# A bilinear einsum on one core: the last weight loads cut by group instead of by pairs of groups

## The chip, the cores and the metric
The kernel runs on one core of one Trainium2 chip. The metric is device time in microseconds (us). Before the change it is a median of 86.06 us over 8 runs, from 85.73 to 86.56. The profile was taken of one execution of 85.89 us, whose span from first to last instruction is 84.6 us.

## The reference
```python
batch, dim_i, dim_j, dim_k = 32, 256, 256, 128        # all float32
out[b, k] = sum over i, j of x[b, i] * y[b, j] * weight[k, i, j]
# np.einsum('bi,bj,kij->bk', x, y, weight)
```
The weight is 128 x 256 x 256 floats, 33.6 MB; x, y and the output are small. So every weight is read once from HBM and used for 32 batches.

## The kernel before, in words
**Layout.** The 128 values of k are split into 32 groups (G) of four: group g holds k = kk * 32 + g for kk from 0 to 3. The 256 values of i are split as i = ip * 8 + ic, with ip from 0 to 31 and ic from 0 to 7. A partition of SBUF holds one pair (ip, kk), 128 in all. In a partition, a group is a row of 8 x 256 values, column block ic holding the 256 values of j for that i. In HBM such a row is contiguous, 8 KB of float32; the load casts it to bf16, so it takes 4 KB in SBUF. A whole group is 1 MB in HBM and 512 KB in SBUF. The profile's sizes of loads are those in SBUF.

**Loads.** Groups 0 and 16 (FIRST) come as float32 on SyncE's queue and are cast by ScalarE. All other groups come through the DMA queue of GpSimd (POOL), in the order of the table LOADS (lines 17 to 31). An entry (groups, lo, hi) is one DMA (line 150): for each of these groups, the column blocks lo to hi - 1 of all 128 partitions. It has one descriptor row for each partition and group, of (hi - lo) x 256 values, and its own semaphore, which all 16 DMA engines raise. All loads are issued in one go near the start, with no wait between them, and wait in the queue in that order. The first five entries are whole rows of 2, 4, 8, 8 and 4 groups. The last eight entries bring groups 7, 23, 15 and 31 in column pieces.

**Units.** UNITS (lines 9 to 15) cuts the 32 groups into five units of 16, 8, 4, 2 and 2 groups, and TensorE works through them in this order. For each column block ic it multiplies xblk, which holds x for this ic on a mask by kk, so that the 128 output rows are the pairs (b, kk), with the weights; PSUM accumulates over the eight ic. In the first four units a matmul takes two groups at once (512 columns). In the last unit, groups 15 and 31, each matmul takes one group (256 columns). Units alternate in the direction in which they run over ic; unit (7, 23) runs from ic 7 down to 0, the last from 0 up. The list `steps` (lines 254 to 256) holds the order of matmuls of a unit as (ic, h, o), where h is the place in PSUM and o the group in the unit. Before a matmul, TensorE waits for the semaphores of the loads which bring its operands, if it has not waited for them before (lines 259 to 275). Every wait holds up all that stands behind it on TensorE.

**Behind TensorE.** VectorE multiplies the sums of a unit by y (line 285) and reduces over j (line 289). In the last unit it does both in one instruction for each group (line 294): the first begins when TensorE has raised s_pe after the last matmul of group 15, the second after the last of group 31 (line 276). Then SyncE sends out the 16 KB of results (line 303), and GpSimd clears the semaphores.

Of the kernel before, what the change touches and what calls it, by code (L numbers as in the profile page):

```python
# [19 lines left out]
    (tuple(range(2, 32, 4)), 0, 8),  # L20
    (tuple(range(1, 32, 4)), 0, 8),
    ((3, 11, 19, 27), 0, 8),
    ((7, 23), 4, 8),
    ((7, 23), 0, 4),
    ((15, 31), 0, 3),
    ((15, 31), 3, 5),
    ((15, 31), 5, 6),
    ((15,), 6, 8),
    ((31,), 6, 7),
    ((31,), 7, 8),  # L30
)
# [6 lines left out]
def kernel(  # L38
# [20 lines left out]
    IC = I // IP  # L59
# [113 lines left out]
    def done(ins):  # L173
        nonlocal n_dve
        n_dve += 1
        ins.then_inc(s_dve, 1)
        return n_dve
# [45 lines left out]
    def product(out, lhsT, rhs, first, last, load):  # L223
        return pe.add_instruction(mybir.InstMatmult(  # L224
            name=nc.get_next_instruction_name(), engine=mybir.EngineType.PE,
            ins=[pe.lower_ap(rhs), pe.lower_ap(lhsT)], outs=[pe.lower_ap(out)],
            start_tensor_calc=first, stop_tensor_calc=last,
            tile_size=(P, P), tile_position=(0, 0), ldweights=load,
        ))
# [9 lines left out]
    for u, unit in enumerate(UNITS):  # L239

        n_g = len(unit)
        last = u == len(UNITS) - 1
        n_b = n_g if last else n_g // 2
        if bank + n_b > BANKS:
            bank = 0
        free = max(freed[bank:bank + n_b])
        if free > at_dve:
            pe.wait_ge(s_dve, free)
            at_dve = free

        up = (len(UNITS) - 1 - u) % 2 == 0
        order = range(IC) if up else range(IC - 1, -1, -1)

        steps = [(ic, h, n_g // n_b * h) for ic in order for h in range(n_b)]
        if last:
            steps = steps[:12] + [(6, 0, 0), (7, 0, 0), (6, 1, 1), (7, 1, 1)]
        for n_step, (ic, h, o) in enumerate(steps):
            n = n_g // n_b
            need = []
            for g in unit[o:o + n]:  # L260
                s = sem_of.get((g, ic))
                if s is not None and s.num not in landed:
                    landed.add(s.num)
                    need.append(s)
            for s in need[:-1]:
                pe.wait_ge(s, 16)
            c = product(
                ps[:, bank + h, :n, :],
                xblk[:, ic, :, :].rearrange("p b kk -> p (b kk)"),
                w_sb[:, p0 + o:p0 + o + n, ic * J:(ic + 1) * J],  # L270
                first=(ic == order[0]), last=(ic == order[-1]), load=(held != ic),
            )
            held = ic
            if need:
                c._wait_ge(need[-1], 16)
            if n_step == len(steps) - 1 or (last and n_step == len(steps) - 3):
                n_pe += 1
                c.then_inc(s_pe, 1)
        prod = tmp[:, u % 2, :n_g, :]
        if last:  # L280
            sums = ps[:, bank:bank + n_g, 0, :]
        else:
            sums = ps[:, bank:bank + n_b, :, :].rearrange("p a h j -> p (a h) j")
        if not last:
            t = done(v.tensor_tensor(  # L285
                out=prod, in0=sums, in1=y4.unsqueeze(1).to_broadcast([P, n_g, J]), op=mult,
            )._wait_ge(s_pe, n_pe))
            freed[bank:bank + n_b] = [t] * n_b
            done(v.tensor_reduce(  # L289
                out=acc[:, unit[0]:unit[-1] + 1:unit[1] - unit[0]], in_=prod, axis=AX, op=add,  # L290
            )._wait_ge(s_dve, t))
        else:
            for n, g in enumerate(unit):
                done(v.tensor_tensor_reduce(  # L294
                    out=prod[:, n, :], in0=sums[:, n, :], in1=y4, scale=1.0, scalar=0.0,
                    op0=mult, op1=add, accum_out=acc[:, g:g + 1],
                )._wait_ge(s_pe, n_pe - 1 + n))
        bank += n_b
        p0 += n_g
# [40 lines left out]
```

## Time and profile before
| What | Before |
|---|---|
| time, median of 8 runs | 86.06 us (85.73 to 86.56) |
| profiled execution, and its span | 85.89 us, 84.6 us |
| TensorE matmul, busy | 34.3 us, 136 instructions |
| VectorE, busy | 24.9 us |
| POOL, busy | 10.7 us |
| HBM read | 33.62 MB, 398 GB/s over the span |
| DMA packets | 5728, of them 5200 on POOL's queue |
| packets under 512 B / 2 KB / 8 KB | 416 / 1632 / 5472 |

Busy time of an engine is the sum over its instructions; TensorE's matmuls are pipelined, so it is no measure of how near TensorE is to its limit. A packet's size is counted as it is written to SBUF. The rate in GB/s of a slice or window counts bytes written too, so a load that casts from float32 to bf16 reads twice that rate from HBM. TensorE's granted clock is about half in three of the page's 40 slices, from 61.3 to 67.7 us.

### The profile page before, as it was taken

Reading aid. Unit: us, or ns where it says so; the run is one execution under the profiler, and the core shown is the slowest. Engines: PE = TensorE matmul, PEld = TensorE weight load, DVE = VectorE, ACT = ScalarE, POOL = GpSimd, SP = SyncE. Lnnn points to the kernel's source line nnn. Section 1 sums busy time; section 2 is a strip of 40 time slices with the busy share of each in tenths; the row PEclk is TensorE's granted clock in tenths of the full one; section 3 lists DMA queues with packets and bytes.
Section 4 is the critical chain, followed back from the end, with each engine's and each line's share of the span. In section 5 each row is a group of like instructions: output and inputs, shape, how many; then the busy total and the mean of one; then the engine's idle time right before and its main releaser. Section 6 shows DMA issues by size and latency. Waiting matters only on the chain.

```text
span 84.6 us, 277 instructions
## 1 busy us (share of the span) xinstructions
PE 34.3 (41%) x136; PEld 3.8 (5%) x38; DVE 24.9 (29%) x28; ACT 5.3 (6%) x5; POOL 10.7 (13%) x19
## 2 busy tenths in 40 slices
PE   0000000000000000000099999998009999999560
PEld 0000000000000000000000000000000011123110
DVE  0799600000000000000000000000999910499962
ACT  0637700000000000000000000000000000000000
POOL 0599994000000000000000000000000000000000
PEclk9999999999999999999999999999955589999999
DMA  4999999999999999999999999999999999999940
GB/s 97 409 405 256 215 217 217 215 217 213 215 217 213 215 215 209 211 217 217 215 217 217 215 213 217 215 217 215 211 209 211 217 217 208 192 209 206 193 57 8
DMA packets 5728, 17.91 MB, mean 212 GB/s; under 512 B 416, under 2 KB 1632, under 8 KB 5472
## 3 DMA queue, kind: packets, MB, share of 16 engines
q0 software_dynamic: 5200, 15.73, 94.5%
q1 hardware_dynamic: 432, 2.11, 6.7%
q10 hardware_dynamic: 96, 0.07, 0.3%
HBM read 33.62 MB, written 0.02 MB: 398 GB/s over the span
## 4 chain that ended last, share of the span: by engine, by line
DMA 44%; PE 41%; DVE 6%; POOL 2%; issue 2%; another core or an unknown queue 2%; POOLq 0%
DMA w_sb<-in_weight_dram 44%; PE ps L224 41%; DVE tmp L285 5%; POOL w_sb L150 1%; DVE tmp L294 1%; POOL ident L156 0%; POOL ident L155 0%; POOLq L134 0%; DVE acc L294 0%
## 5 line engine op out<-in xcount | busy, mean ns | idle before, releaser
L224 PE MATMUL ps<-w_sb,xblk 128*128 128x512 bf16 (+1 forms) x136 | 34.3, 414 | 48.3 <-DMA w_sb<-in_weight_dram 43.6
L285 DVE TENSOR_TENSOR tmp<-ps,y 128x4096 f32<-128x4096 f32 (+3 forms) x4 | 8.6, 2153 | 54.2 <-PE ps L224 54.2
L150 POOL DMA_DIRECT2D w_sb<-in_weight_dram x13 | 10.0, 777 | 2.6 <-POOLq L134 2.6
L289 DVE TENSOR_REDUCE acc<-tmp 128x16 f32<-128x4096 f32 (+3 forms) x4 | 8.6, 2154 | 0.1
L224 PEld LDWEIGHTS ps<-w_sb,xblk 128*128 128x128 bf16 x38 | 3.8, 103 | 78.6 <-DMA w_sb<-in_weight_dram 44.7
L165 ACT CAST w_sb<-w_f 128x1024 bf16<-128x1024 f32 x4 | 4.0, 1042 | 2.3 <-DMA w_f<-in_weight_dram 2.3
L214 DVE STREAM_TRANSPOSE y<-y_rep 32x256 f32<-32x256 f32 x4 | 1.7, 435 | 0.1
L185 DVE STREAM_TRANSPOSE xt<-x_rep 32x256 f32<-32x256 f32 x4 | 1.7, 434 | 0.1
L197 DVE TENSOR_SCALAR xblk<-xt,mask 128x256 bf16<-128x256 f32 x4 | 1.5, 524 | 0.0
L179 DVE COPY x_rep<-x_sb 32x1024 f32<-32x1024 f32 x1 | 0.7, 681 | 2.6 <-PEq L134 2.6
L165 ACT ACT_TABLE_LOAD x1 | 1.3, 1283 | 2.6 <-PEq L134 2.6
L294 DVE CUSTOM_DVE_ANT_0 tmp<-ps,y 128x256 f32<-128x256 f32 x2 | 0.8, 424 | 0.8 <-PE ps L224 0.8
L209 DVE COPY y_rep<-yt 32x1024 f32<-32x1024 f32 x1 | 0.7, 694 | 0.0
L206 DVE STREAM_TRANSPOSE yt<-y_sb 32x256 f32<-32x256 f32 x1 | 0.4, 426 | 0.0
L192 DVE TENSOR_REDUCE mask<-ident 128x4 f32<-128x128 f32 x1 | 0.4, 376 | 0.1
L156 POOL TENSOR_SCALAR_AFFINE_SELECT ident<-ident 128x128 f32<-128x128 f32 x1 | 0.3, 287 | 0.1
L155 POOL MEMSET ident<- 128x128 f32 x1 | 0.2, 223 | 0.0
L294 DVE DVE_READ_ACCUMULATOR2_ANT acc<- 128x1 f32 x2 | 0.2, 83 | 0.0
L324 POOL MEMSET const-float32-0.0<- 128x1 f32 x1 | 0.1, 98 | 0.2 <-issue 0.2
L324 POOL MEMSET const-bfloat16-1.0<- 128x1 bf16 x1 | 0.1, 101 | 0.0
L324 POOL MEMSET const-uint8-127<- 128x1 uint8 x1 | 0.1, 101 | 0.0
L324 POOL MEMSET const-float32-1.0<- 128x1 f32 x1 | 0.1, 98 | 0.0
## 6 DMA issues: line engine op xcount, KB each, us to landing
w_sb<-in_weight_dram POOLq DMA_DIRECT2D x2, 4096.0 KB, 46.2
w_sb<-in_weight_dram POOLq DMA_DIRECT2D x2, 2048.0 KB, 41.2
w_f<-in_weight_dram SPq DMA_DIRECT2D x2, 1024.0 KB, 6.5
w_sb<-in_weight_dram POOLq DMA_DIRECT2D x1, 1024.0 KB, 9.7
w_sb<-in_weight_dram POOLq DMA_DIRECT2D x2, 512.0 KB, 66.7
w_sb<-in_weight_dram POOLq DMA_DIRECT2D x1, 384.0 KB, 68.8
w_sb<-in_weight_dram POOLq DMA_DIRECT2D x1, 256.0 KB, 69.4
w_sb<-in_weight_dram POOLq DMA_DIRECT2D x2, 128.0 KB, 69.5
```

The costliest lines, as they stand in the source:

```text
L150: pool.dma_start(out=w_of(groups)[:, :, lo * J:hi * J], in_=rows_of(groups)[:, :, lo * J:hi * J],).then_inc(s, 16)
L165: c = act.copy(out=w_sb[:, place_of[g], lo:hi], in_=w_f[:, n, lo:hi])
L179: t = done(v.tensor_copy(out=x_rep, in_=x_sb.rearrange("b (ip ic) -> b ic ip", ic=IC).unsqueeze(3) .to_broadcast([B, IC, IP, KK]),)._wait_ ...
L185: c = v.transpose(out=xt[q * 32:(q + 1) * 32, :, :], in_=x_rep[:, :, q * IP // Q:(q + 1) * IP // Q, :],)
L192: t = done(v.tensor_reduce(out=mask, in_=ident.rearrange("p (ip kk) -> p kk ip", kk=KK), axis=AX, op=add,)._wait_ge(s_pool, 2))
L197: c = v.tensor_scalar(out=xblk[:, :, :, kk], in0=xt, scalar1=mask[:, kk:kk + 1], scalar2=None, op0=mult,)
L209: t = done(v.tensor_copy(out=y_rep, in_=yt.unsqueeze(3).to_broadcast([B, J // 32, B, KK]),)._wait_ge(s_dve, t))
L214: c = v.transpose(out=y4[q * 32:(q + 1) * 32, :].rearrange("p (jb j) -> p jb j", j=32), in_=y_rep[:, :, q * BQ:(q + 1) * BQ, :],)
L224: return pe.add_instruction(mybir.InstMatmult(name=nc.get_next_instruction_name(), engine=mybir.EngineType.PE, ins=[pe.lower_ap(rhs), pe.l ...
L285: t = done(v.tensor_tensor(out=prod, in0=sums, in1=y4.unsqueeze(1).to_broadcast([P, n_g, J]), op=mult,)._wait_ge(s_pe, n_pe))
L289: done(v.tensor_reduce(out=acc[:, unit[0]:unit[-1] + 1:unit[1] - unit[0]], in_=prod, axis=AX, op=add,)._wait_ge(s_dve, t))
L294: done(v.tensor_tensor_reduce(out=prod[:, n, :], in0=sums[:, n, :], in1=y4, scale=1.0, scalar=0.0, op0=mult, op1=add, accum_out=acc[:, g:g ...
```

## The change
The first five loads stay. The other eight become ten: each of them brings columns of one group alone, four column blocks at a time for groups 7, 23, 15 and for the first half of 31; the second half of 31 comes as two blocks, one and one. The order of TensorE in the last unit is fitted to this: ic 0 to 3 for both groups in turn, then ic 4 to 7 of group 15, then ic 4 to 7 of group 31. The signal to VectorE that group 15 is done moves with it, from the third matmul before the end to the fifth, both counted so that the last is the first. Arithmetic, bytes and the number of matmuls stay as they are.

```diff
@@ LOADS
     ((3, 11, 19, 27), 0, 8),
-    ((7, 23), 4, 8),
-    ((7, 23), 0, 4),
-    ((15, 31), 0, 3),
-    ((15, 31), 3, 5),
-    ((15, 31), 5, 6),
-    ((15,), 6, 8),
+    ((7,), 4, 8),
+    ((23,), 4, 8),
+    ((7,), 0, 4),
+    ((23,), 0, 4),
+    ((15,), 0, 4),
+    ((31,), 0, 4),
+    ((15,), 4, 8),
+    ((31,), 4, 6),
     ((31,), 6, 7),
     ((31,), 7, 8),
 )
@@ tile_einsum_bilinear_kernel
         if last:
-            steps = steps[:12] + [(6, 0, 0), (7, 0, 0), (6, 1, 1), (7, 1, 1)]
+            steps = steps[:8] + [(ic, h, h) for h in range(2) for ic in range(4, IC)]
@@
-            if n_step == len(steps) - 1 or (last and n_step == len(steps) - 3):
+            if n_step == len(steps) - 1 or (last and n_step == len(steps) - 5):
```

## The prediction
> **What bounds the kernel now.** I read four views of the kernel before: the page's chain by line, the chain in order of time, the windows around the landings, and the waits. The page says that weight loads and TensorE share the chain almost evenly:
>
> ```profile
> span 84.6 us, 277 instructions
> DMA w_sb<-in_weight_dram 44%; PE ps L224 41%; DVE tmp L285 5%; POOL w_sb L150 1%; DVE tmp L294 1%; POOL ident L156 0%; POOL ident L155 0%; POOLq L134 0%; DVE acc L294 0%
> ```
>
> That share misleads about the end. In order of time, the last stretch of the chain reads (start us, duration us, what):
>
> ```profile
> 75.85 2.38 PE ps L224 x11
> 78.22 0.44 another core or an unknown queue
> 78.66 0.04 issue
> 78.70 0.81 PE ps L224 x6
> 79.52 0.47 another core or an unknown queue
> 79.99 0.05 issue
> 80.03 0.61 PE ps L224 x4
> 80.64 0.02 issue
> 80.66 0.39 PE ps L224 x2
> 81.06 0.50 another core or an unknown queue
> 81.56 0.05 issue
> 81.60 0.64 PE ps L224 x3
> 82.24 0.04 another core or an unknown queue
> 82.28 0.05 issue
> 82.33 0.30 PE ps L224
> 82.62 0.02 issue
> 82.65 0.42 DVE tmp L294
> ```
>
> The reader is to see that TensorE has caught up at 78.22. From there it stands still before each piece of groups 15 and 31; the waits view over the same stretch names w_sb<-in_weight_dram as what it waited for. On one core, "unknown queue" is therefore the load. A landing is the end of such a wait: 78.66, 79.99, 81.56, 82.28 (and 80.64 and about 81.91, by the starts of the weight loads that wait, at 80.66 and 81.95). After the last landing comes a fixed tail: 0.05 issue, 0.30 matmul, 0.45 on VectorE, the output DMA to 84.6. So the end is the last landing plus 2.3 us, and the stream of loads bounds it. Windows over the stream (stretch, its length, five engines' busy time, TensorE clock, DMA share, GB/s written to SBUF):
>
> ```profile
> 61.60:71.40 9.80, 7.85 (x26) 0.73 (x6) 6.26 (x2) 0.00 (x0) 0.00 (x0) 0.65 1.07 214
> 76.80:78.70 1.90, 1.42 (x7) 0.45 (x5) 1.90 (x2) 0.00 (x0) 0.00 (x0) 1.00 1.19 204
> 78.70:80.00 1.30, 0.81 (x6) 0.19 (x2) 1.27 (x3) 0.00 (x0) 0.00 (x0) 1.00 1.33 192
> 80.60:81.60 1.00, 0.44 (x3) 0.10 (x2) 0.76 (x2) 0.00 (x0) 0.00 (x0) 1.00 0.55 67
> 81.60:82.30 0.70, 0.64 (x3) 0.21 (x3) 0.27 (x1) 0.00 (x0) 0.00 (x0) 1.00 0.08 10
> ```
>
> Full rows move at 214 GB/s. With short rows the rate falls to 192, and in the last 1.7 us only about 0.07 MB moves: most of the 16 DMA engines are done by 80.6, a few stragglers set the last landing.
>
> **What the Trainium skill says.** "DMA: Bandwidth & Descriptors", section "Why a DMA increments its semaphore by 16 and not by 1": the full count means that the slowest of the engines is done. The two windows above agree: share 0.55 and then 0.08 while TensorE still waits. The same page, "Anatomy of one DMA — SWDGE (gpsimd) path", gives about 2 us fixed per DMA, mostly completion latency. The trace agrees that this is no serial price: the last pieces land 0.35 and 0.37 us apart. "Why small descriptors are slow (HBM only)" has a fixed overhead per packet; the fall from 214 to 192 GB/s points the same way.
>
> **The sum before.** The last full-row load (groups 3, 11, 19, 27) is issued at 7.7 us and lands 63.7 later, at 71.4; both numbers are in the answer for line 150. The pieces of 7 and 23 (issued at 8.4 and 9.1, landing after 65.8 and 67.6) land at about 74.25 and 76.75. At 214 GB/s, 512 KB takes 2.45 us, 384 KB 1.84, 256 KB 1.22, 128 KB 0.61, 64 KB 0.31. Time from landing to landing, less that:
> - 7 and 23: 2.85 - 2.45 = 0.40, and 2.50 - 2.45 = 0.05.
> - 15 and 31: 1.91 - 1.84 = 0.07; 1.33 - 1.22 = 0.11; 0.65 - 0.61 = 0.04; 0.92 - 0.61 = 0.31; 0.35 - 0.31 = 0.04; 0.37 - 0.31 = 0.06.
>
> The 2 MiB took 10.88 us against 9.80 at full rate. The excess of 1.08 us is all that a new cut of the same bytes can act on: 0.45 in 7 and 23, 0.63 in 15 and 31.
>
> **The change part by part.** (1) Groups 7 and 23: two loads of 256 rows become four of 128, rows of 2 KB as before, same bytes. Nothing is saved; two more piece ends are added. Between nothing and 0.11 each, the dearest plain step above; I take 0.03 each (the cheap steps show 0.04 to 0.06 with short rows as well): +0.06. I leave the 0.40 at the first of them where it is, since row length and place stay.
>
> (2) Groups 15 and 31: six loads of 256+256+256+128+128+128 = 1152 rows become six of 768 (three of 2 KB, one of 1 KB, two of 512 B). If the 0.63 goes with rows, it is 0.55 ns a row, and 768 rows leave 0.42: -0.21. Bounds: nothing (it belongs to ends and stragglers; the final two pieces are unchanged), and -0.63 (all vanishes).
>
> (3) TensorE. The order view has the same 120 matmuls of 512 columns and 16 of 256; two more weight loads (12 in place of 10 in the last unit, 0.10 each, beside matmuls), and two more waits on semaphores in unit (7, 23), whose loads have landed by 76.75 when their last columns are wanted after 77. In the last unit the second of the first eight matmuls now needs group 31's first half, and six stand behind it. By bytes it lands after six pieces of 1.22 us, 71.4 + 7.32 + 0.45 to 0.6 of excess = about 79.3. These seven run at some 0.11 each (six took 0.81, with 0.28 the latency of one): done at 80.2. Group 15's second half lands at about 80.55; four matmuls, done at 81.15. The two of piece (31, 4:6), landing near 81.2, are done by 81.6, ahead of the last two landings near 81.6 and 82.1. Cover: the waits themselves; at nothing. With that cover gone a late matmul costs 0.11.
>
> (4) VectorE. It is busy with units 1 to 3 until 81.40 (its reduction at 80.71 for 0.69). Group 15's product and sum (0.42 + 0.08, overlapped to 0.45) began at 82.03 and ended at 82.46, just 0.19 before group 31's at 82.65. Now it can begin at 81.4 to 81.5 and end by 81.95. No gain while the last landing governs; it merely keeps VectorE out of the way.
>
> (5) POOL issues 15 loads in place of 13, at 0.55 to 0.71 each, until about 14.5 us in place of 13.6. What it issues last lands after 80 us; POOL is next wanted at 83.5. Nothing. Two more semaphores are cleared by a range operation, beside the output DMA's 1.1 us wait; nothing.
>
> Sum on the profiled execution (85.89, span 84.6): +0.06 - 0.21 = -0.15, last landing 82.28 to 82.13, span 84.45, time 85.74. The profiled execution lies 0.17 under the median of 86.06; against the median the forecast is 85.9.
>
> **Rivals.** (A) *The stragglers go.* If short rows cause the uneven finish, halving the pieces of 512 B evens the engines. The 0.07 MB left at 80.6 spread over all engines would need 0.35 us more, so in the limit the end comes about 1 us earlier; half of it gives 85.5. For: share 0.55 and 0.08 come right after the shortest rows. Against: the final two pieces stay, and one lag of 0.40 was there with 2 KB rows.
>
> (B) *Ends of single-group pieces are dear (slower).* Place: the stream, from 71.4 on. The three single-group pieces of before cost 0.31 + 0.04 + 0.06, 0.14 each. If that goes with having one group, the new stream has ten such pieces: 1.4 us against 1.08, +0.3, time 86.4; with 0.2 each, +0.9, 87.0. It decides from 0.11 per piece. For: the largest step of the tail is the first single-group piece. Against: the next two cost 0.04 and 0.06, and the two full-row loads of single groups on SP's queue ran at the top rate of slices 2 and 3 (405 to 409 GB/s).
>
> (C) *TensorE's or VectorE's order binds instead.* Group 31 now has eight matmuls that wait for a later landing than before. It needs the half of 31 about 1.5 us later than estimated; then up to +0.2: 86.2. Little speaks for it.
>
> (D) *The load was never limited by its cut:* stragglers stay, and it is 86.06, no difference.
>
> **How the numbers follow.** Forecast (small gain, -0.3 to 0) 0.34; D 0.15; A 0.29; B 0.18; C 0.04. Within 0.5% is 0.43 us, about what a measurement of this kernel can tell from no change (the eight runs spread over 0.83). Of its 0.34 the forecast gives 0.07 to faster, A gives 0.27; B gives 0.15 to slower, C and D 0.03 by scatter: faster 0.34, same 0.48, slower 0.18. Range: A down to 85.35, B up to 86.5; beyond are the outer ends of A and B, a tenth each. The likeliest case's own range is 85.7 to 86.1.
>
> **What would show it.** Packets: 5728 - 384 + 32 = 5376, under 2 KB 896 in place of 1632. Step 1: landings of the four pieces of 7 and 23 some 1.22 to 1.6 apart, the last near 76.8. Step 2: from there to the last landing, 5.3 us in place of 5.53. Step 3: TensorE waits before the matmuls of 31's first half near 79.3 and still waits for each of the last three pieces. Step 4: group 15's product starts before 81.6. Wrong would be: a last landing outside 81.9 to 82.4, or a chain whose end hangs on VectorE or on TensorE's own work rather than on a load.

## The result, and the profile after

The changed kernel takes 85.13 us (median of 11 runs, 84.85 to 85.80) against 86.03 us before (median of 32 runs). The ratio is 0.9898 with a 95% interval from 0.9876 to 0.9919: about 0.9 us faster. The forecast was 85.9 us, in a range from 85.35 to 86.5. The direction was right; the gain is six times the 0.15 us that was worked out, and it lies outside the range.

The profiled execution of after is one of its two slowest, 85.81 us, and that hides the gain at first sight. From the page of after: the span, the granted TensorE clock in 40 slices (in tenths of full speed), the DMA packets, and the chain by line.

```profile
span 84.5 us, 283 instructions
PEclk9999999999999999999999999999965999999659
DMA packets 5376, 17.91 MB, mean 212 GB/s; under 512 B 448, under 2 KB 896, under 8 KB 5120
DMA w_sb<-in_weight_dram 44%; PE ps L226 39%; DVE tmp L287 5%; POOL w_sb L152 1%; DVE tmp L296 1%; POOL ident L158 0%; POOL ident L157 0%; POOLq L136 0%; DVE acc L296 0%
```

The counts of packets are those forecast (5376, of them 896 under 2 KB). The clock has a dip at slices 38 and 39 that before has not; its line reads:

```profile
PEclk9999999999999999999999999999955589999999
```

The end of the chain of after, in order of time (start us, duration us, what):

```profile
75.94 0.74 another core or an unknown queue
76.68 0.05 issue
76.73 1.04 PE ps L226 x4
77.76 0.12 another core or an unknown queue
77.88 0.04 issue
77.93 0.27 PE ps L226
78.19 0.95 another core or an unknown queue
79.14 0.04 issue
79.18 3.35 PE ps L226 x15
82.54 0.03 issue
82.56 0.42 DVE tmp L296
82.99 0.01 DVE acc L296
```

As before, an "unknown queue" is a wait for a load. The last wait ends at 79.14, when the first half of group 31 lands. Then 15 matmuls take 3.35 us with no further wait between them: in this execution TensorE has become the last link. The windows of after over the same stretches as those shown of before, and one more (stretch, length, five engines' busy time, TensorE clock, DMA share, GB/s):

```profile
61.60:71.40 9.80, 8.69 (x32) 0.78 (x7) 5.38 (x3) 0.00 (x0) 0.00 (x0) 0.83 1.06 214
76.80:78.70 1.90, 1.23 (x5) 0.23 (x4) 1.79 (x3) 0.00 (x0) 0.00 (x0) 1.00 1.13 210
78.70:80.00 1.30, 0.82 (x5) 0.26 (x3) 0.52 (x1) 0.00 (x0) 0.00 (x0) 0.60 1.13 199
80.60:81.60 1.00, 1.00 (x7) 0.70 (x5) 0.00 (x0) 0.00 (x0) 0.00 (x0) 0.50 0.30 37
81.60:82.30 0.70, 0.70 (x5) 0.33 (x3) 0.43 (x2) 0.00 (x0) 0.00 (x0) 0.50 0.00 0
```

Two things are to be seen. The stream ends earlier: nothing moves after 81.6, where before still had a share of 0.08, and the rates on the way are 210 and 199 GB/s for 204 and 192. The last load is issued at 13.2 and lands 68.6 us later, at 81.7 (81.74 by the unrounded times), for 82.3 before. And TensorE's clock is 0.60 and then 0.50 behind its wait of 0.95 us. With the tail of before (0.05 + 0.30 + 0.45) a landing at 81.74 would have ended VectorE's work at 82.54; it ended at 83.0. So this execution gained 0.54 us in the stream and gave nearly all of it back on TensorE, at half clock. Kernels 3 and 4 below keep the full clock and show the gain whole.

One more view is used below, the trace's packet records. A packet on POOL's queue has a usual duration by its size in SBUF: 324 ns for 4 KB, 173 for 2 KB, 135 for 1.5 KB, 98 for 1 KB, 60 for 512 B. I call a packet a *stumble* when it takes over 20 ns more; those of the first 16 us, at the start of the stream, are left aside. Before has 26 stumbles between 72.1 and 73.1 us (2.6 us in all, over 16 engines) and 19 between 79.5 and 81.0 (1.9 us). After has 11 at the first place (0.9 us) and none at the second. A load has landed when the last of the 16 DMA engines has raised its semaphore. For the last load of before the first engine does so at 81.00, the middle one at 81.19 and the last at 82.28; in after they do so at 80.97, 81.09 and 81.74. So most engines are done at the same time in both, and what before loses it loses at its slowest engines.

### The profile page after: what moved, and what is told of

It reads as the page before. It is cut to its first block, busy times and chain, and to the rows that moved or that the text cites. A ratio compares the mean times of both kernels' runs of the same rounds, so it can differ in the third digit from the quotient of the medians.

```text
span 84.5 us, 283 instructions
## 1 busy us (share of the span) xinstructions
PE 33.1 (39%) x136; PEld 4.4 (5%) x40; DVE 25.0 (30%) x28; ACT 5.3 (6%) x5; POOL 10.9 (13%) x21
## 2 busy tenths in 40 slices
DMA packets 5376, 17.91 MB, mean 212 GB/s; under 512 B 448, under 2 KB 896, under 8 KB 5120
## 4 chain that ended last, share of the span: by engine, by line
DMA 44%; PE 39%; DVE 6%; another core or an unknown queue 3%; POOL 2%; issue 2%; POOLq 0%
DMA w_sb<-in_weight_dram 44%; PE ps L226 39%; DVE tmp L287 5%; POOL w_sb L152 1%; DVE tmp L296 1%; POOL ident L158 0%; POOL ident L157 0%; POOLq L136 0%; DVE acc L296 0%
## 5 line engine op out<-in xcount | busy, mean ns | idle before, releaser
L226 PE MATMUL ps<-w_sb,xblk 128*128 128x512 bf16 (+1 forms) x136 | 33.1, 408 | 49.4 <-DMA w_sb<-in_weight_dram 44.8
L226 PEld LDWEIGHTS ps<-w_sb,xblk 128*128 128x128 bf16 x40 | 4.4, 112 | 77.6 <-DMA w_sb<-in_weight_dram 43.7
```

What stands on the lines that cost most here:

```text
L226: return pe.add_instruction(mybir.InstMatmult(name=nc.get_next_instruction_name(), engine=mybir.EngineType.PE, ins=[pe.lower_ap(rhs), pe.l ...
```

## The experiments

All ratios are to runs of the kernel before beside them on the same chip. In short diffs the first five loads are left out where nothing is changed in them.

**1. The new loads with the old order of matmuls.**

```diff
# against after
-            steps = steps[:8] + [(ic, h, h) for h in range(2) for ic in range(4, IC)]
+            steps = steps[:12] + [(6, 0, 0), (7, 0, 0), (6, 1, 1), (7, 1, 1)]
...
-            if n_step == len(steps) - 1 or (last and n_step == len(steps) - 5):
+            if n_step == len(steps) - 1 or (last and n_step == len(steps) - 3):
```

> The ten loads of after, but the last unit's matmuls in the order of before. Theory R (fewer and longer rows in 15 and 31 let the stragglers catch up) and theory G (a piece of two groups is dear in itself) both say that the gain is in the stream: 85.1 to 85.3 against 86.0 before. Theory O (the order of the last unit's matmuls gives the gain): no better than 85.8.

Measured: 85.41 us, ratio 0.9914 (0.9888 to 0.9940). The gain is in the stream. The time is just above the 85.1 to 85.3 expected. The new order of matmuls adds little, and that little can't be told from noise here. This profile kept its full clock: the last landing is at 13.2 + 68.5 = 81.7, and no stumble is behind 73.3 us.

**2. Only 7 and 23, and 3. only 15 and 31.**

```diff
# 2, against before
-    ((7, 23), 4, 8),
-    ((7, 23), 0, 4),
+    ((7,), 4, 8),
+    ((23,), 4, 8),
+    ((7,), 0, 4),
+    ((23,), 0, 4),
# 3, against after
-    ((7,), 4, 8),
-    ((23,), 4, 8),
-    ((7,), 0, 4),
-    ((23,), 0, 4),
+    ((7, 23), 4, 8),
+    ((7, 23), 0, 4),
```

> Only groups 7 and 23 are loaded one group at a time; 15 and 31 and the order of matmuls as before. Theory R: rows keep their length, so no difference, 85.9 to 86.1. Theory G: the excess of 0.40 us at the first piece of 7 and 23 shrinks to about 0.1, so 85.7.

> Only groups 15 and 31 are loaded as after, with its order of matmuls; 7 and 23 in two pieces of two groups as before. Theory R: the whole gain, 85.1 to 85.3. Theory G: some half of it, 85.5 to 85.6, the excess of 0.40 us stays at the first piece of 7 and 23.

Measured: 86.08 us for 2, ratio 0.9985 (0.9968 to 1.0003), no difference. 85.22 us for 3, ratio 0.9901 (0.9874 to 0.9928), the whole gain. The chain of 3 shows how a tail looks when the clock stays up:

```profile
80.62 0.04 issue
80.67 0.63 PE ps L224 x3
81.29 0.06 another core or an unknown queue
81.35 0.05 issue
81.40 0.30 PE ps L224
81.69 0.02 issue
81.72 0.43 DVE tmp L294
```

The last landing is at 81.35, 0.9 us before that of the kernel before (82.28), and the tail behind it is the same as there. Not all of the 0.9 lies in the loads that were changed: the last piece of 7 and 23, which this kernel loads as before does, lands at 76.20 here and at 76.77 in before. One execution of each is too little to divide the gain; more profiles are compared under step 2 below.

**4. The row lengths of after, but in pairs of groups where it can be.**

```diff
# against after
-    ((7,), 4, 8),
-    ((23,), 4, 8),
-    ((7,), 0, 4),
-    ((23,), 0, 4),
-    ((15,), 0, 4),
-    ((31,), 0, 4),
+    ((7, 23), 4, 8),
+    ((7, 23), 0, 4),
+    ((15, 31), 0, 4),
```

> Row lengths of after in every column, but columns 4 to 7 and 0 to 3 of 7 and 23, and 0 to 3 of 15 and 31, come in pieces of two groups; the last four pieces as after. Theory R: as after, 85.1 to 85.3, or a little better for its three pieces fewer. Theory G: 0.3 to 0.5 us slower than after, 85.5 to 85.7.

Measured: 85.02 us, ratio 0.9885 (0.9858 to 0.9911). As fast as after. So "one group in place of two" is not what helps in the pieces that were changed here; what helps is in the last four pieces, which kernel 4 shares with after.

**5 to 8. Rows and packets, early and late.** Kernel 5 puts 33 more packets on every engine ahead of the tail. Kernels 6 and 8 put a run of 64 rows of 512 B on every engine, early and late. Kernel 7 takes short rows away.

```diff
# 5, against after
-    ((3, 11, 19, 27), 0, 8),
+    ((3, 11, 19, 27), 0, 4),
+    ((3, 11, 19, 27), 4, 8),
# 6, against after
-    ((7,), 4, 8),
-    ((23,), 4, 8),
-    ((7,), 0, 4),
-    ((23,), 0, 4),
+    ((7, 23), 7, 8),
+    ((7, 23), 6, 7),
+    ((7, 23), 5, 6),
+    ((7, 23), 4, 5),
+    ((7, 23), 0, 4),
# 7, against after
-    ((7,), 4, 8),
-    ((23,), 4, 8),
-    ((7,), 0, 4),
-    ((23,), 0, 4),
-    ((15,), 0, 4),
-    ((31,), 0, 4),
+    ((7, 23), 0, 8),
+    ((15, 31), 0, 4),
# 8, against after
-    ((15,), 4, 8),
-    ((31,), 4, 6),
+    ((15,), 4, 5),
+    ((15,), 5, 6),
+    ((15,), 6, 7),
+    ((15,), 7, 8),
+    ((31,), 4, 5),
+    ((31,), 5, 6),
```

> After, with the load of groups 3, 11, 19 and 27 cut in two halves of 2 KB rows: 33 more packets on each DMA engine ahead of the tail (336 in all; before has 325, after 303), and none of them short. Theory S (a long run of short rows at the end is what makes single engines stumble): as after, 85.1 to 85.3. Theory N (the place in the queue does it: in before the long packets begin some 292 packets in, and after ends soon behind that place): the stumbles are back in the last pieces, 85.7 to 86.0.

> Columns 7, 6, 5 and 4 of groups 7 and 23 come one by one, two groups each: 64 rows of 512 B in a run on each DMA engine, ahead of the unchanged tail of after (352 packets in all). Theory S: the stumbles come in this run, at 72 to 75 us, and none in the tail; what single engines lose there stays lost, 85.6 to 86.2. Theory N: they come in the tail, from the 292nd packet on, when rows are 2 KB long again.

> Groups 7 and 23 in one load of whole rows, columns 0 to 3 of 15 and 31 in one load of two groups, the last four pieces as after: 283 packets on each engine. Theory S: short rows are the same as in after, so 85.0 to 85.2; if the loss at about 72.6 us that all kernels show so far goes with the step from 4 KB to 2 KB rows, it moves to about 77 us and the time stays, and if it goes with the place in the queue it is hidden and gives some 0.1 to 0.2 us. Theory N: no worse than after, 84.9 to 85.1.

> After, with columns 4 to 7 of 15 and of 31 one by one: the last 64 rows on each engine are all of 512 B (after has 16 of them behind 8 of 1 KB), 339 packets in all. Theory S: stumbles as in before or worse, 85.8 to 86.4. If neither short rows nor the number of packets matter, 85.2 to 85.4 (six piece ends more).

Measured: 5 takes 85.44 us, ratio 0.9920 (0.9893 to 0.9947); its profile has no stumble at all behind 16 us. 6 takes 90.77 us, ratio 1.0554 (1.0511 to 1.0597). 7 takes 84.78 us, 0.9866 (0.9829 to 0.9903), no stumble either. 8 takes 85.31 us, 0.9923 (0.9892 to 0.9953), and no stumble behind 73.3 us, although its last 64 rows on every engine are of 512 B.

Both theories fall: S wanted stumbles in 8, N wanted them in 5. Kernel 5 is a little slower than the 85.3 expected; its profile has TensorE at half clock over the tail, see step 3 below. The number of packets (336 in kernel 5) is harmless, and a run of short rows is harmless in 8 and costs 4.8 us against before in 6. Two differences between 6 and 8 are left: pairs against single groups, and early against late.

**9 and 10. Pairs and places exchanged.**

```diff
# 9, against kernel 6
-    ((7, 23), 7, 8),
+    ((7,), 7, 8),
+    ((23,), 7, 8),
-    ((7, 23), 6, 7),
+    ((7,), 6, 7),
+    ((23,), 6, 7),
...
# 10, against before
-    ((7, 23), 4, 8),
-    ((7, 23), 0, 4),
-    ((15, 31), 0, 3),
...
-    ((31,), 7, 8),
+    ((7,), 4, 8),
+    ((23,), 4, 8),
+    ((7,), 0, 4),
+    ((23,), 0, 4),
+    ((15, 31), 0, 4),
+    ((15, 31), 4, 5),
+    ((15, 31), 5, 6),
+    ((15, 31), 6, 7),
+    ((15, 31), 7, 8),
```

> The run of 512 B rows of the early-short-rows kernel (90.8 us), in the same place of the queue and in as many rows, but each piece of one group alone: eight pieces of 8 rows on each engine in place of four of 16. Theory P (short rows are dear only in pieces of two groups): the loss of 4.7 us is gone, 85.0 to 85.6. Theory E (short rows are dear where many loads are still queued behind them, and free at the end of the queue): still 89 to 91.

> The late-short-rows kernel (85.3 us) turned into pairs: columns 0 to 3 of 15 and 31 in one piece of two groups, columns 4, 5, 6 and 7 each in one piece of two groups with 512 B rows; 7 and 23 as after, the last matmuls in the order of before. Theory P: some 4 us slower than before, 88 to 91. Theory E: no stumbles, 85.4 to 86.0 (both products of the last unit now come behind the last landing, some 0.5 us).

Measured: 9 takes 90.75 us, ratio 1.0553 (1.0503 to 1.0602): single groups, and no better than pairs. 10 takes 86.88 us, 1.0123 (1.0080 to 1.0166): late, and yet it stumbles, 65 times behind 78.5 us. Neither theory explains both. What 6, 9 and 10 share, and 8 doesn't, is the order of columns: rows of two groups that follow one another read the *same* narrow column, while 8 goes through the columns of one group and then of the other.

**11 and 12. The cuts of before, with one piece or all pieces in single groups.**

```diff
# 11, against before
-    ((15, 31), 5, 6),
+    ((15,), 5, 6),
+    ((31,), 5, 6),
# 12, against before: 11, and also
-    ((15, 31), 0, 3),
-    ((15, 31), 3, 5),
+    ((15,), 0, 3),
+    ((31,), 0, 3),
+    ((15,), 3, 5),
+    ((31,), 3, 5),
```

> Before, with one piece alone split: column 5 of groups 15 and 31 (512 B rows) comes as two pieces of one group. Theory P: that piece was where the stumbles began, so most of the gain of after, 85.2 to 85.5. Theory E, or any that goes by rows or packets: as before, 85.9 to 86.2.

> Before, with all pieces of 15 and 31 split into pieces of one group, at the same columns: the same 1152 rows of the same lengths, nine pieces in place of six. Theory P: the whole gain of after or nearly, 85.1 to 85.5. Theory R of the prediction (0.55 ns for each row): no gain, 85.9 to 86.2.

Measured: 85.91 us, ratio 0.9986 (0.9967 to 1.0005), and 85.93 us, 0.9995 (0.9978 to 1.0012). No gain from either. That is against the theory of pairs, and agrees with the one of neighbours: 15 and 31 still follow one another at each column.

**13 and 14. Only the order of equal pieces.** Kernel 9 has the columns 5 and 4 split as the two shown. Kernel 13 is 9 with its eight short pieces in another order. Kernel 14 is 8 with its last eight pieces in another order, and with the matmuls in the order of before.

```diff
# 13: order of the eight pieces of 512 B rows
-    7: col 7   23: col 7   7: col 6   23: col 6   7: col 5   23: col 5   7: col 4   23: col 4
+    7: col 7   7: col 6   7: col 5   7: col 4   23: col 7   23: col 6   23: col 5   23: col 4
# 14: order of the last eight pieces
-    15: col 4   15: col 5   15: col 6   15: col 7   31: col 4   31: col 5   31: col 6   31: col 7
+    15: col 4   31: col 4   15: col 5   31: col 5   15: col 6   31: col 6   15: col 7   31: col 7
```

> The eight single-group pieces of 512 B rows in place of the first half of 7 and 23, as in the kernel that took 90.75 us, in another order alone: columns 7, 6, 5, 4 of group 7 and then those of group 23, in place of column 7 of both, column 6 of both and so on. Theory C (two pieces in a row that read the same column of their rows, so that all 16 engines are at the same column at once, are what is dear): 85.3 to 87. Theory E (short rows are dear wherever many packets are queued behind them): 90 to 91 as before.

> The late-short-rows kernel (85.31 us, no stumbles in its tail) with its last eight pieces in the order by column: column 4 of 15 and of 31, column 5 of both, and so on; the matmuls in the order of before. Theory C: stumbles from 78 us on, the last landing 0.8 to 1.3 us later than its 82.04, 86.0 to 86.8. Theory E: 85.2 to 85.6.

Measured: 13 takes 86.83 us, ratio 1.0045 (1.0020 to 1.0070), where 9 had 1.0553 (each against before on its own chip). 14 takes 86.72 us, 1.0045 (1.0027 to 1.0062), where 8 had 0.9923. The windows of 9 while its short rows pass:

```profile
71.00:72.00 1.00, 1.00 (x6) 0.09 (x1) 0.00 (x0) 0.00 (x0) 0.00 (x0) 1.00 0.60 30
72.00:73.00 1.00, 1.00 (x7) 0.20 (x2) 0.72 (x1) 0.00 (x0) 0.00 (x0) 1.00 1.06 69
73.00:74.00 1.00, 1.00 (x6) 0.20 (x2) 1.00 (x1) 0.00 (x0) 0.00 (x0) 1.00 1.15 81
```

and those of 13:

```profile
71.00:72.00 1.00, 1.00 (x7) 0.10 (x1) 0.00 (x0) 0.00 (x0) 0.00 (x0) 1.00 1.26 163
72.00:73.00 1.00, 1.00 (x6) 0.10 (x1) 0.18 (x1) 0.00 (x0) 0.00 (x0) 1.00 1.26 151
73.00:74.00 1.00, 1.00 (x6) 0.19 (x2) 1.00 (x1) 0.00 (x0) 0.00 (x0) 1.00 1.28 171
```

Same rows, same lengths, same place in the queue: 30, 69 and 81 GB/s in one order, 163, 151 and 171 in the other. From 72 to 74 us the DMA share in 9 is 1.06 and more at about a third of 214 GB/s: the engines have packets in flight and are slow at them. In the first of the three stretches the share is only 0.60 (and 0.38 in kernel 6), so for a good part of it engines have no packet in flight at all. Behind 68 us, 9 has 251 stumbles that sum to 41 us over the engines, 13 has 54 that sum to 3.7. Kernel 6 loses as much time as 9 with 153 stumbles that sum to 14.6 us, so slow packets are not the whole of the loss there; what holds the engines between packets is open. And the order doesn't make short rows free at this place: 13 is still 1.5% above after (ratios 1.0045 and 0.9898). The last load lands at 16.0 + 70.9 = 86.9 in 9 and at 15.9 + 66.7 = 82.6 in 13. Late in the queue, the windows of 8 and then of 14:

```profile
78.90:79.70 0.80, 0.41 (x4) 0.19 (x2) 0.77 (x2) 0.00 (x0) 0.00 (x0) 1.00 1.43 185
79.70:80.60 0.90, 0.90 (x8) 0.39 (x4) 0.17 (x1) 0.00 (x0) 0.00 (x0) 1.00 1.43 189
```

```profile
78.90:79.70 0.80, 0.80 (x8) 0.31 (x4) 0.80 (x2) 0.00 (x0) 0.00 (x0) 1.00 1.25 149
79.70:80.60 0.90, 0.66 (x4) 0.10 (x1) 0.75 (x2) 0.00 (x0) 0.00 (x0) 1.00 1.38 156
```

Here the order is worth 1.0 us of last landing (15.2 + 66.8 = 82.0 and 15.2 + 67.8 = 83.0). From there to the end of VectorE's work 14 takes 0.98 us and 8 takes 0.80: the order of matmuls of 14 brings both products of the last unit behind the last landings, and its clock is at half there. So some 0.2 us of 14's loss is not in the stream.

**15 and 16. The same at the cuts of before.**

```diff
# 15, against 12: two neighbours exchanged
-    ((31,), 3, 5),
     ((15,), 5, 6),
+    ((31,), 3, 5),
     ((31,), 5, 6),
     ((15,), 6, 8),
# 16, against 15: the last neighbour of the same columns moved away
     ((15,), 5, 6),
+    ((15,), 6, 8),
     ((31,), 3, 5),
     ((31,), 5, 6),
-    ((15,), 6, 8),
     ((31,), 6, 7),
```

> The kernel with all the cuts of before in single groups (85.93 us), with two neighbours exchanged: columns 3 to 4 and column 5 of group 15, then those of group 31, so that no two pieces with rows of 1 KB or less that follow one another read the same column. Theory C: the gain of after or most of it, 85.2 to 85.5. If it is the number or length of the rows: 85.8 to 86.0 as without the exchange.

> The nine single-group pieces at the cuts of before, once more in another order: after columns 0 to 2 of both groups come columns 3 to 4, 5, 6 to 7 of group 15, then 3 to 4, 5, 6 and 7 of group 31. The exchange before this one left columns 6 to 7 of 15 beside column 6 of 31, and its stumbles stood just there, at 80.46 to 81.17. Rows, lengths and number of pieces are the same. Theory C: no stumbles behind 78 us, ratio to before 0.990 to 0.993. If rows or the number of packets (328) count: 0.995 to 1.0.

Measured: 15 takes 85.84 us, ratio 0.9951 (0.9933 to 0.9970). That is half the gain, less than I had expected. What I had overlooked: columns 6 to 7 of 15 still stood beside column 6 of 31, and its stumbles are there and nowhere else behind 73 us. 16 takes 85.71 us, 0.9934 (0.9909 to 0.9959), with no stumble behind 73.1 us; the ratio is just above the 0.990 to 0.993 expected. Its windows against those of 12 (12 first):

```profile
80.60:81.60 1.00, 0.27 (x1) 0.00 (x0) 0.00 (x0) 0.00 (x0) 0.00 (x0) 1.00 0.66 83
81.60:82.30 0.70, 0.56 (x3) 0.21 (x3) 0.13 (x1) 0.00 (x0) 0.00 (x0) 1.00 0.13 16
```

```profile
80.60:81.60 1.00, 0.80 (x7) 0.51 (x5) 0.28 (x1) 0.00 (x0) 0.00 (x0) 0.94 0.54 70
81.60:82.30 0.70, 0.68 (x4) 0.10 (x1) 0.41 (x2) 0.00 (x0) 0.00 (x0) 0.50 0.00 0
```

The stream ends before 81.6 in 16, as in after, and is still at work behind it in 12, as in before. Nine pieces and 1152 rows are the same in both, though the order of row lengths is not; in 9 and 13, and in 8 and 14, all rows of the pieces that change places have one length. Kernel 15 also speaks against a rival, that it is dear to go from one group to the other and back: it does so from column 5 of 15 to column 3 of 31, and from column 5 of 31 to column 6 of 15, without a stumble, and stumbles only from 80.46 us, where column 6 of 31 follows columns 6 and 7 of 15.

The account has a limit: columns 3 and 4 of 15 and 31 (1 KB rows) follow one another in before and in 2, 11 and 12, and none of their 256 rows stumbles in any of these four. The stumbles begin with the 512 B rows of column 5. So the same column in two pieces running was dear here with 512 B rows and behind them, and not by itself.

What 16 lacks to after is not in the stream (its own clock of 0.50 at the end adds to it): its chain ends with two products of VectorE in a row, at 81.89 and 82.32, since the order of matmuls of before needs columns 4 and 5 of group 31 before it finishes group 15.

**17 and 18. A better kernel.** Whole rows for group 15 too, and then one piece end less.

```diff
# 17, against 7
-    ((15, 31), 0, 4),
-    ((15,), 4, 8),
+    ((15,), 0, 8),
+    ((31,), 0, 4),
...
-            steps = steps[:8] + [(ic, h, h) for h in range(2) for ic in range(4, IC)]
+            steps = [(ic, h, h) for h in range(2) for ic in range(IC)]
...
-            if n_step == len(steps) - 1 or (last and n_step == len(steps) - 5):
+            if n_step == len(steps) - 1 or (last and n_step == len(steps) - 9):
# 18, against 17
-    ((31,), 4, 6),
-    ((31,), 6, 7),
+    ((31,), 4, 7),
```

> One step on from the kernel with whole rows for 7 and 23 (84.78 us): group 15 whole as well, then columns 0 to 3, 4 to 5, 6 and 7 of group 31; the last unit does all of group 15 before group 31. Fewer and longer rows, no two neighbours of the same column but whole rows: every theory says no worse, 84.6 to 84.9, if TensorE is not late with its last eight matmuls.

> The kernel with whole rows for 7, 23 and 15, with columns 4 to 6 of group 31 in one piece in place of 4 to 5 and 6: one piece end less. TensorE then has three matmuls between the last two landings, 0.3 us apart. 84.8 to 85.0, ratio to before 0.984 to 0.987: no difference from it.

Measured: 84.90 us, ratio 0.9843 (0.9812 to 0.9874), and 84.87 us, 0.9858 (0.9822 to 0.9894). Both beat before by 1.4 to 1.6% and, with kernel 7 (0.9866), lie below after's 0.9898. The interval of 17 lies just below that of after. None of the three was timed beside after, and their intervals overlap each other, so which of them is best stays open.

## Why the prediction was right and wrong

**What bounds the kernel: right.** The end of the stream governs: the last landing moved from 82.28 to 81.35 in kernel 3, and the time followed by the same 0.9 us. The excess over the 9.80 us at full rate, all that a new cut could act on, had the right size. From the landing of groups 3, 11, 19 and 27 to the last landing the trace of before has 10.90 us, that of after 10.32 and that of kernel 3 10.10, so 0.6 and 0.8 us came out of it.

**Step 1, pieces of 7 and 23, +0.06: right in substance.** Kernel 2, which makes this part alone, has a ratio of 0.9985 (0.9968 to 1.0003). A piece end costs nothing that can be seen. In after the last of these pieces landed at 76.68, for 76.8 forecast.

**Step 2, 15 and 31, -0.21: the step that failed.** The 0.63 us of excess was spread over rows at 0.55 ns each, and the part of the rows that stay was kept. That price per row is what failed. Kernels 12 and 16 have the same 1152 rows, of the same lengths, and differ by the order of pieces: ratios 0.9995 and 0.9934. Kernel 8 has 1280 rows in 15 and 31, after 768, and like after no stumble in them. The excess sat in the stumbles of a few engines, which came where two pieces in a row, or both groups of one piece, read the same narrow column. Before has this at column 5 of both groups (512 B rows) and at columns 6 and 7. The change takes it away at a stroke because, past columns 0 to 3, it reads all of 15 and then all of 31. The term was not -0.21 but near its lower bound, -0.63. From the landing of the last piece of 7 and 23 to the last of all, the trace of before has 5.51 us, and those of kernels 2, 11 and 12, with the same neighbours at the tail, 6.12, 5.62 and 5.98; those of after and of kernels 1, 3, 4 and 5 have from 5.06 to 5.15. The means are 0.7 us apart. So the profiled execution of before had a mild tail, and a sum made on it alone was bound to be small. Two things stay open: the 0.2 us between these 0.7 and the gain of 0.9, and how much of it the fewer rows of after give, for kernel 16, which has the order without them, shows two thirds of after's gain and loses some of the rest to its matmuls.

**Step 3, TensorE covered by the waits: right in place, wrong in cost.** The wait for 31's first half ended at 79.14, for 79.3 forecast. What was not priced is that the wait there is 0.95 us, longer than any at the tail of before, and that TensorE's clock was 0.50 from 79.0 to 82.4 in the profiled execution. That cost nearly 0.5 us and is why this profile shows what was named as a sign of error, a chain that ends on TensorE's own work. (The other sign, a last landing outside 81.9 to 82.4, is there too, at 81.74, by step 2.) Kernel 5, with the same tail, shows the low clock too (15 matmuls in 3.37 us); kernels 3, 4 and 7 keep a clock of 1.00 over the tail. The long wait alone does not lower the clock: kernels 1, 3 and 8 have it as well, 0.94 to 0.98 us, and keep 1.00 up to the end of their matmuls. What decides it is not shown. In the 3.41 us before the drop TensorE was busy for 1.70 us in after and 1.31 in kernel 5; but kernel 14 dropped behind 1.9 us of work in such a stretch, and kernel 10 kept its clock behind 1.6.

**Step 4, VectorE: not decided by this profile.** Group 15's product began at 81.73 rather than before 81.6, behind the slow matmuls; in kernel 3 it began at 80.66, well ahead.

**Step 5, POOL: right.** The last load was issued at 13.2, POOL was done at 13.9 (for 14.5 forecast), and nothing waited for it.

**The rivals.** A, the stragglers go, was the true one, for a wrong reason: it laid them to 512 B rows, and kernel 8 has 64 of those in a row without a stumble. Its time in the limit, 1 us earlier, was nearly reached (its own figures, 0.35 us of bytes behind 80.6, would have given 1.3), and the price I gave it was half of that. B falls: ten single-group pieces cost nothing (kernels 1 and 2). C came true in the profiled execution alone, by the clock and not by a late landing; the median shows no loss from it. D falls with the interval of the result. The fault in the range was to let A, at 0.29, reach down to 85.35 alone.

## What to carry to other kernels

When the end of a stream sets the end of the kernel, look at where single DMA engines lose time, not only at the mean rate: an excess over the full rate that is spread evenly on paper can sit in a few places. If a matrix's rows have to be loaded in column pieces, finish the columns of one block of rows before those of the next, and don't send two pieces with the same narrow column (here rows of 512 B in SBUF) one after the other; early in the queue this order alone was worth some 4 us, late in it 1. Whole rows wherever the consumer can wait for them are simpler still, and were as good as anything here.

## What the runs showed of the hardware that was not expected

The order of equal loads changes their rate by a factor of two: 69 against 151 GB/s from 72 to 73 us, in kernels 9 and 13. By the layout all 128 rows of a piece lie a multiple of 8 KB apart in HBM, so such a neighbour keeps all engines at the same offset within 8 KB. That this is the reason is argued and not shown, and so is what is short then. Why the same exchange costs 4.3 us of last landing early in the queue and 1.0 late is open too.

The other place of stumbles, at 72.1 to 73.1 us, is in before, in after and in most of the others, some 226 packets into each engine's queue. It is absent in the profiles of kernels 5, 7, 17 and 18, and small in 14 (6 stumbles, 0.3 us). Its cause was not found; in before the piece that lands next comes 0.4 us later than at the full rate.
